# Output projection whole for token blocks 0 to 3 and in two chunks for 4 to 7, with three MLP pairs ahead and two side by side

## The chip, the cores and the metric

The kernel runs on one NeuronCore of a Trainium2 chip. Its time is the device time of one execution in microseconds (us), as the median of several runs. The engines have an instruction queue each and work side by side: TensorE (PE in the profile, its weight loads PEld), VectorE (DVE), ScalarE (ACT), GpSimd (POOL); SyncE (SP) issues the DMA transfers. The program puts the instructions of each engine in one order, and one that waits holds up those behind it on its engine.

## The reference

Two residual layers over 1024 tokens of width 1024, all in float32. Layer 0 mixes with two recurrences, layer 1 with windowed attention; each mixer ends in a projection `m = y @ w_out`, and each layer has an MLP.

```python
for layer in range(DEPTH):                       # DEPTH = 2
    un = rmsnorm(h, g[0])
    m = rec_mixer(un, ...) if layer % 2 == 0 else window_attention(un, ...)
    # both end in: y (1024 x 1024) @ w_out (1024 x 1024)
    h = h + rmsnorm(m, g[1])
    u = rmsnorm(h, g[2])
    m = jnp.square(jax.nn.relu(u @ w1)) @ w2     # w1: 1024 x 4096, w2: 4096 x 1024
    h = h + rmsnorm(m, g[3])
```

## The kernel before

Each large product keeps the precision of float32 by splitting both operands into a rounded high part and the rest (`split`, L84 to L86: ScalarE copies into the rounded type, VectorE subtracts). Three matmuls stand for one: high by high, high by low, low by high. A split therefore costs one ScalarE and one VectorE instruction on each tile, and these two engines prepare what TensorE multiplies.

**Output projection** (`out_proj`). The contraction over 1024 features is cut into 8 tiles k. `hid[k]` is the split transposed mixer output `ys[k]`, `ws[k]` the split weight rows k. For each of 8 blocks b of 128 tokens and each half c of the output columns, `g2_block` (L209) accumulates the products in one PSUM bank. In layer 0, `ys[4]` to `ys[7]` come from the four heads of one of the recurrences, in layer 1 `ys[6]` and `ys[7]` from the last group of attention heads; these are the last to be finished. So the work is in two chunks: k = 0 to 3 for all 8 blocks (12 matmuls for each half block, 192 in all), which can run between the mixer's own matmuls, and then k = 4 to 7 for all 8 blocks. Chunk one is evacuated by ScalarE to `acc` (blocks 0 to 3) or to `far` (blocks 4 to 7, in tiles `ax`, which are copied to `acc` by DMA once `yp` has room); chunk two is added to it by VectorE (L288).

**Norms behind it** (`make_tail`). For each finished block, `add_norm` multiplies by the gain on GpSimd (`mg`, L236), takes the mean square on ScalarE (`junk`, L147) and a Newton step in small VectorE instructions (L148 to L152), adds the residual (`hb`, L238), stores it, and norms it again for the MLP (L147 and then L185, which writes `acc` anew). `turn` transposes a block on TensorE (L191, 8 matmuls of 128 columns into two `aux` banks) and splits it as an operand of the MLP (`xh`, `xl`, and a float32 copy `xf`). Blocks 0 to 3 are turned here, blocks 4 to 7 in the MLP.

**MLP, first product** (`strassen_in`). Hidden columns are handled in 16 pairs p of 128-column slabs. Each pair is a two-by-two Strassen scheme (Winograd's form) of seven products i, each of 12 matmuls of 512 columns. Products 1 and 2 need tokens 0 to 511 only (`p1`, `p2`), the others sums of quarters of the weights (`lead_sums`, `sum_op`, `half`) and of the activations (`acts[3]` to `acts[7]`). Activations 3 and 6 need blocks 4 to 7 turned (`turn_far`), 5 and 7 more sums over them. So the first `lead` pairs do products 1 and 2 while `turn_far` goes on; then their products follow in the order 6, 7, 5, 4, 3 (`rest`). From pair 2 on, a pair runs through 1, 6, 2, 7, 5, 4, 3 while the operands of the next pair are made (`prep_step`).

**PSUM.** Eight banks: two of tag `m0`, two of `m1`, four of `aux`. The out projection uses the `m` banks in turn; `p1` holds an `aux` bank for its pair until `p2` has added product 2 and ScalarE has read it, and every half of a turn takes an `aux` bank.

**Order.** The order of code gives priorities, from which a list scheduler sets the order on every engine at build time; it inserts the semaphores. The mixers have their steps in a string (`REC_ORDER`: `S3` is a stage of head 3, `G3` the gate projection of head 3, `O3` its output). Tiles come from pools: `wp` holds `raw` (2 buffers of freshly loaded weights) and `w1` (3 buffers of split weights), `xp` 8 tiles of 8 KB a partition, `yp` 8 of 4 KB; the pools "op" and "mlp1" are opened and closed in turn over the same memory as the mixers' pools, so a tile of a new pool waits for the last reader of the memory below it.

Of the kernel before, what the change touches and what calls it, by code (L numbers as in the profile page):

```python
# [8 lines left out]
F32 = mybir.dt.float32  # L9
# [9 lines left out]
P = 128  # L19
# [20 lines left out]
             "Z2 G2 S2 z2 s2 G3 !O2 z3 V3 Q3 S3 s3 O3")  # L40
# [11 lines left out]
def trunk_kernel(ctx, tc, x, norm_g, rec_w_in, rec_conv_w, rec_conv_b, rg_w_r, rg_b_r, rg_w_i,  # L52
# [199 lines left out]
    def out_proj(ys, w, h_src, h_dst, layer, nxt, pre):  # L252
# [21 lines left out]
        with phase("op") as pool:  # L274
# [12 lines left out]
            def evac(sl, o):  # L287
                return V.tensor_tensor(acc[b][:, sl], o, acc[b][:, sl], op=ALU.add)  # L288
# [17 lines left out]
    def mlp(xt, hgs, layer, h_src, h_dst, nxt, pre):  # L306
# [3 lines left out]
        def strassen_in(pool):  # L310
# [66 lines left out]
            def prep_step(p, slot):  # L377
# [923 lines left out]
```

## Time and profile before

| | us |
|---|---|
| median of 3 runs | 2274.64 (2272.72 to 2275.8) |
| the profiled execution's own time | 2273.52 |
| its span in the trace | 2271.8 |
| TensorE busy in the span | 2174.1 (96%) |
| VectorE busy | 1728.0 (76%) |
| ScalarE busy | 1145.0 (50%) |
| GpSimd busy | 223.1 (10%) |

TensorE is busy for 96% of the span and for all of the long stretches of the MLPs. A matmul's end is modelled, so the busy share of TensorE is an upper bound; how much a stretch loses is read from the number of matmuls in it and the pace at which they run where nothing waits. A row of the timeline gives the start, the length, engine, line, operation, tiles and shape, how many instructions were merged, and in brackets the engine's idle time before it and what ended it. A row of the table by stretches gives the stretch, its length, then for each engine its busy time and its instructions in it, the clock that TensorE was granted, the DMA share and GB/s.

### The profile page before, as it was taken

Reading aid. Unit: us, or ns where it says so; the run is one execution under the profiler, and the core shown is the slowest. Engines: PE = TensorE matmul, PEld = TensorE weight load, DVE = VectorE, ACT = ScalarE, POOL = GpSimd, SP = SyncE. Lnnn points to the kernel's source line nnn. Section 1 sums busy time; section 2 is a strip of 40 time slices with the busy share of each in tenths; the row PEclk is TensorE's granted clock in tenths of the full one; section 3 lists DMA queues with packets and bytes.
Section 4 is the critical chain, followed back from the end, with each engine's and each line's share of the span. In section 5 each row is a group of like instructions: output and inputs, shape, how many; then the busy total and the mean of one; then the engine's idle time right before and its main releaser. Section 6 shows DMA issues by size and latency. Waiting matters only on the chain. (4 is left out here: it accounts for less than half of the span.)

```text
span 2271.8 us, 28186 instructions
## 1 busy us (share of the span) xinstructions
PE 2174.1 (96%) x10392; PEld 1790.7 (79%) x10392; DVE 1728.0 (76%) x2941; ACT 1145.0 (50%) x1812; POOL 223.1 (10%) x128
## 2 busy tenths in 40 slices
PE   8999999998899999999999888989899999999998
PEld 8878888887788888888878666767678888888886
DVE  6697767758866665778887888997986666578887
ACT  6566445544544456333344665765554445533342
POOL 0230000003000000000022244211200000000003
PEclk9999999999999999999999999999999999999999
DMA  5111011143444446444344112114334443744433
GB/s 148 53 33 56 29 29 30 46 139 121 135 153 153 151 141 255 145 152 153 114 148 125 33 38 56 33 33 152 132 135 153 153 153 136 245 138 153 153 118 129
DMA packets 180764, 264.03 MB, mean 116 GB/s; under 512 B 17041, under 2 KB 98961, under 8 KB 180625
## 3 DMA queue, kind: packets, MB, share of 16 engines
q1 hardware_dynamic: 180624, 262.22, 35.2%
q8 instruction: 82, 1.34, 0.3%
q14 instruction: 58, 0.47, 0.1%
HBM read 179.87 MB, written 70.78 MB: 110 GB/s over the span
## 5 line engine op out<-in xcount | busy, mean ns | idle before, releaser
L116 PE MATMUL m<-xh,w1hl 128*128 128x512 f32 (+1 forms) x1472 | 431.8, 372 | 0.0
L116 PEld LDWEIGHTS m<-xh,w1hl 128*128 128x128 f32 x1472 | 268.9, 193 | 38.1 <-ACT xh L204 0.2
L116 PE MATMUL m<-xl,w1hl 128*128 128x512 f32 (+1 forms) x736 | 274.1, 373 | 0.5 <-DVE xl L205 0.5
L236 POOL TENSOR_TENSOR mg<-acc,g 128x1024 f32<-128x1024 f32 x32 | 82.5, 2577 | 1695.1 <-DVE acc L553 1210.8
L86 DVE TENSOR_TENSOR w1hl<-raw,w1hl 128x1024 fp32r<-128x1024 f32 x108 | 135.9, 1259 | 107.0 <-ACT w1hl L85 106.9
L418 PE MATMUL aux<-xh,w1hl 128*128 128x512 f32 x512 | 169.0, 392 | 0.0
L418 PE MATMUL m<-xh,w1hl 128*128 128x512 f32 x512 | 168.0, 390 | 0.0
L418 PE MATMUL m<-xh,ws 128*128 128x512 f32 x512 | 167.8, 389 | 0.0
L567 ACT ACTIVATE hidh<-hidl 128x1536 fp32r<-128x1536 f32 (+1 forms) x56 | 89.5, 1598 | 145.1 <-DMA hidl<-hs 145.1
L644 PE MATMUL m<-w2h,hidh 128*128 128x512 f32 x416 | 161.8, 389 | 0.0
L644 PE MATMUL m<-w2l,hidh 128*128 128x512 f32 x416 | 161.8, 389 | 0.0
L644 PE MATMUL m<-w2h,hidl 128*128 128x512 f32 x416 | 161.8, 389 | 0.0
L116 PEld LDWEIGHTS m<-xl,w1hl 128*128 128x128 f32 x736 | 142.3, 193 | 19.7 <-DVE xl L205 0.8
L568 DVE TENSOR_TENSOR hidl<-hidl,hidh 128x1536 fp32r<-128x1536 f32 (+1 forms) x56 | 105.9, 1891 | 54.4 <-ACT hidh L567 54.4
L85 ACT ACTIVATE w1hl<-raw 128x1024 fp32r<-128x1024 f32 x116 | 122.4, 1056 | 40.7 <-DMA raw<-in_mlp_w_dram 21.3
L85 ACT ACTIVATE w2h<-b 128x1536 fp32r<-128x1536 f32 (+1 forms) x48 | 76.7, 1599 | 103.7 <-PE m L644 60.6
L85 ACT ACTIVATE ws<-s 128x512 fp32r<-128x512 f32 x88 | 55.7, 634 | 144.6 <-PE m L418 87.2
L644 PE MATMUL aux<-w2h,hidh 128*128 128x512 f32 x312 | 121.4, 389 | 0.0
L644 PE MATMUL aux<-w2l,hidh 128*128 128x512 f32 x312 | 121.4, 389 | 0.0
L644 PE MATMUL aux<-w2h,hidl 128*128 128x512 f32 x312 | 121.4, 389 | 0.0
L418 PEld LDWEIGHTS aux<-xh,w1hl 128*128 128x128 f32 x512 | 96.6, 189 | 20.3 <-ACT u L434 0.4
L418 PEld LDWEIGHTS m<-xh,w1hl 128*128 128x128 f32 x512 | 96.2, 188 | 20.3 <-ACT xh L85 0.4
(298 smaller groups left out, 5152.9 us busy)
## 6 DMA issues: line engine op xcount, KB each, us to landing
hidl<-hs SPq DMA_DIRECT2D x42, 768.0 KB, 4.5
raw<-in_mlp_w_dram SPq DMA_DIRECT2D x30, 1024.0 KB, 5.5
hs<-hid SPq DMA_DIRECT2D x104, 256.0 KB, 2.1
b<-in_mlp_w_dram SPq DMA_DIRECT2D x24, 768.0 KB, 4.8
raw<-in_rec_w_in_dram SPq DMA_DIRECT2D x28, 512.0 KB, 3.7
hidl<-hs SPq DMA_DIRECT2D x14, 1024.0 KB, 5.6
hs<-u SPq DMA_DIRECT2D x52, 256.0 KB, 2.0
hres<-hb SPq DMA_DIRECT2D x24, 512.0 KB, 2.7
```

Of the source, the lines that this page charges most:

```text
L85: A.activation(hi, src, AF.Copy)
L86: (eng or V).tensor_tensor(lo, src, hi, op=ALU.subtract)
L116: T.matmul(o[:, c0:c0 + nw], a[:, k, :], b[k // 4][half][:, k % 4, c0:c0 + nw], start=(n == 0), stop=(n == 3 * KT - 1))
L236: G.tensor_tensor(mg, m, g_post, op=ALU.mult)
L418: T.matmul(o, a[:, k, :], b[:, k, :], start=(first and n == 0), stop=(n == 11), skip_group_check=not first)
L567: A.activation(h, f32(l), AF.Copy)
L568: V.tensor_tensor(l, f32(l), h, op=ALU.subtract)
L644: T.matmul(o, a_[:, j, sl], b_[:, j, :], start=(not more and n == 0), stop=(n == last), skip_group_check=more)
```

## The change

- Output projection: chunk one (k = 0 to 3) is done ahead for blocks 4 to 7 only. Then blocks 0 to 3 are done whole (24 matmuls for each half block, evacuated by ScalarE, no addition on VectorE), and last blocks 4 to 7 get their chunk two. `hid[4]` and `hid[5]` have free tiles early. The copies through `ax` are gone.
- The split weights of the MLP's first slabs are prefetched for three pairs, after block 3; blocks 0 to 3 are turned behind blocks 4 to 6.
- MLP: `lead` is 3. Products 1 and 2 of pairs 0, 1 and 2 run while blocks 4 to 7 are turned. Pairs 0 and 1 then do their remaining products side by side, in the order 3, 5, 6, 7, 4 (`side_by_side`), each product of both pairs behind the making of its operand. Activations 5 and 6 are split in one instruction over 2048 columns each, 6 no longer block by block. The raw weights of pairs 0 and 1 go to tiles of the pool "mlp1" (tags `xh_7`, `xl_7`).
- `G3` moves behind `S3` in the recurrence's order.

The number of TensorE instructions is the same. On VectorE, 16 additions of chunk two are gone (8 in each layer) and 8 splits of 512 columns are replaced by 2 of 2048; ScalarE has 8 evacuations more to `hid` and the same number of out-projection evacuations. SP has 8 transfers less through `ax`.

```diff
-             "Z2 G2 S2 z2 s2 G3 !O2 z3 V3 Q3 S3 s3 O3")
+             "Z2 G2 S2 z2 s2 !O2 z3 V3 Q3 S3 G3 s3 O3")
...
+        def copy(sl, o):
+            return A.activation(acc[b][:, sl], o, AF.Copy)
+
+        def add(sl, o):
+            return V.tensor_tensor(acc[b][:, sl], o, acc[b][:, sl], op=ALU.add)
...
-        acc = [yp.tile([P, D], F32, tag="y", name=f"acc{b}") for b in range(4)]
-        far = []
-        for i in range(2):
-            t = xp.tile([P, 2, S], F32, tag="x", name=f"ax{i}")
-            far += [t[:, b, :] for b in range(2)]
+        acc = {b: yp.tile([P, D], F32, tag="y", name=f"acc{b}") for b in range(4, NB)}
         ws = [load_wo(k, wp, "w1", 3) for k in range(3)] + [load_wo(3, xp, "x", 8)]
-        for b in range(NB):
-            dst = acc[b] if b < 4 else far[b - 4]
-            g2_block(b, [hid[k] for k in range(4)], ws, lambda sl, o: A.activation(dst[:, sl], o, AF.Copy))
+        for b in range(4, NB):
+            g2_block(b, [hid[k] for k in range(4)], ws, copy)
         with phase("op") as pool:
...
-            for b in range(4, NB):
-                acc.append(yp.tile([P, D], F32, tag="y", name=f"acc{b}"))
-                Y.dma_start(acc[b], far[b - 4])
-            ws = [load_wo(k, pool, "wo", 4) for k in range(4, KT)]
-            prefetch(pre)
+            ws += [load_wo(k, pool, "wo", 4) for k in range(4, KT)]
+            acc.update({b: yp.tile([P, D], F32, tag="y", name=f"acc{b}") for b in range(4)})
...
             for b in range(NB):
-                ins = g2_block(b, [hid[k] for k in range(4, KT)], ws, evac)
+                if b < 4:
+                    ins = g2_block(b, [hid[k] for k in range(KT)], ws, copy)
+                else:
+                    ins = g2_block(b, [hid[k] for k in range(4, KT)], ws[4:], add)
                 if b >= 1:
                     add_norm(b - 1, ins)
-                if 2 <= b < 6:
-                    turn(b - 2)
+                if b == 3:
+                    prefetch(pre)
+                if b == 4:
+                    turn(0)
+                if 4 <= b < 7:
+                    turn(b - 3)
...
             def load(p):
...
+                if p < 2:
+                    t = pool.tile([P, KT, 2 * P], F32, tag="x" + "hl"[p] + "_7", name="raw2")
                 else:
...
             def turn_far(b):
...
                 p4 = turned(hgs[b], 1)
-                V.tensor_tensor(t2[:, :, blk], p4, t1[:, :, blk], op=ALU.subtract)
                 A.activation(h3, p4, AF.Copy)
                 V.tensor_tensor(l3, p4, h3, op=ALU.subtract)
-                split(h6, l6, t2[:, :, blk])
+                V.tensor_tensor(t2[:, :, blk], p4, t1[:, :, blk], op=ALU.subtract)
...
+            def side_by_side(p, i):
+                t = temps[p]
+                u2, u3 = t[:, half_s[0]], t[:, half_s[1]]
+                c = lambda h, s: outs[p][h][:, half_s[s]]
+                o = banks[p] if i == 4 else mm_ps({3: "m1", 5: "m0", 6: "aux", 7: "m1"}[i])
+                banks[p] = o
+                product(o, p, i, i != 4, True)
+                if i == 3:
+                    A.activation(c(0, 1), o, AF.Copy)
+                elif i == 5:
+                    outs[p].append(yp.tile([P, S], F32, tag="y", name="hid1"))
+                    A.activation(c(1, 1), o, AF.Copy)
+                    V.tensor_tensor(c(0, 1), o, c(0, 1), op=ALU.add)
+                elif i == 6:
+                    V.tensor_tensor(u2, o, u2, op=ALU.add)
+                    V.tensor_tensor(c(0, 1), c(0, 1), u2, op=ALU.add)
+                    relu2(p, 0, 1, None)
+                elif i == 7:
+                    V.tensor_tensor(u3, o, u2, op=ALU.add)
+                    V.tensor_tensor(c(1, 1), c(1, 1), u3, op=ALU.add)
+                    relu2(p, 1, 1, None)
+                else:
+                    V.tensor_tensor(c(1, 0), o, u2, op=ALU.add)
+                    relu2(p, 1, 0, None)
+                    store(p)
...
-            lead = 2
+            lead, both = 3, (0, 1)
             for p in range(lead):
                 pre_a(p)
-            load(0)
+            for p in both:
+                load(p)
             lead_sums(0)
+            sum_op(0, 3)
...
             p1(0)
+            p1(1)
             turn_far(4)
-            p1(1)
+            p2(0)
             turn_far(5)
-            p2(0)
-            load(1)
-            sum_op(0, 6)
+            p2(1)
             turn_far(6)
-            p2(1)
+            lead_sums(1)
+            sum_op(1, 3)
+            p1(2)
             turn_far(7)
-            lead_sums(1)
-            sum_op(1, 6)
-            for p in range(lead):
-                rest(p, 1)
...
+            p2(2)
+            for p in both:
+                side_by_side(p, 3)
+            act_tiles(5)
+            split(*acts[5], t1)
...
+            for p in both:
+                side_by_side(p, 5)
+            act_tiles(6)
+            split(*acts[6], t2)
...
                            layer, (layer, 2),
-                           [(mlp_w1[layer], 2 * j * P) for j in range(2)])
+                           [(mlp_w1[layer], 2 * j * P) for j in range(3)])
```

What the scheduler makes of it is shown at three places. In these rows the number behind a name tells tiles apart: `m_13512` is a PSUM bank's tile of one half block, `hx_13390` and `hx_13393` are `hid[4]` and `hid[5]` of layer 1, `hidh`/`hidl` are `hid[6]` and `hid[7]`, `wohl` the split weights k = 4 to 7, `w1hl` and `xhl` in the out projection those of k = 0 to 3.

TensorE behind the last attention matmul of layer 1 (`aux<-pl,vs`), before:

```order
L1178 MATMUL aux<-pl,vs 128x512
L216 MATMUL m_13437<-w1hl,hx_13262 128x512
L216 MATMUL m_13437<-w1hl,hx_13265 128x512 x3
L216 MATMUL m_13437<-xhl,hx_13268 128x512 x3
L216 MATMUL m_13451<-w1hl,hx_13259 128x512 x3
L216 MATMUL m_13451<-w1hl,hx_13262 128x512 x3
L216 MATMUL m_13451<-w1hl,hx_13265 128x512 x3
L216 MATMUL m_13451<-xhl,hx_13268 128x512 x3
```

The same place now:

```order
L1211 MATMUL aux<-pl,vs 128x512
L216 MATMUL m_13512<-w1hl,hx_13242 128x512 x3
L216 MATMUL m_13512<-w1hl,hx_13245 128x512 x3
L216 MATMUL m_13512<-xhl,hx_13248 128x512 x3
L216 MATMUL m_13434<-wohl,hx_13390 128x512
L216 MATMUL m_13460<-wohl,hx_13390 128x512
L216 MATMUL m_13486<-wohl,hx_13390 128x512
L216 MATMUL m_13512<-wohl,hx_13390 128x512
L216 MATMUL m_13434<-wohl,hx_13390 128x512 x2
```

Before, 67 matmuls of chunk one (7 of `m_13437`, then 60 of five further half blocks) stand there ahead of the first use of `wohl`; now 9 do, and the four open half blocks of blocks 0 and 1 then take k = 4 to 7 in turns.

ScalarE in layer 1, from the split of `hid[6]` on, before:

```order
L85 ACTIVATE hidh<-y_9688 128x1024
L85 ACTIVATE wohl<-raw 128x1024
L85 ACTIVATE hidh<-y_9689 128x1024
L273 ACTIVATE ax_13275<-m_13451 128x512
L85 ACTIVATE wohl<-raw 128x1024
L273 ACTIVATE ax_13276<-m_13465 128x512
L85 ACTIVATE hx_13524<-y_9686 128x1024
```

The same place now:

```order
L85 ACTIVATE hidh<-y_9668 128x1024
L85 ACTIVATE wohl<-raw 128x1024
L85 ACTIVATE hidh<-y_9669 128x1024
L85 ACTIVATE wohl<-raw 128x1024 x3
L264 ACTIVATE acc_13424<-m_13434 128x512
L264 ACTIVATE acc_13424<-m_13460 128x512
```

The splits of `hid[4]` and `hid[5]` have moved ahead, to between the attention units; the order of `hid[6]`, `hid[7]` and the four `wohl` is kept.

VectorE in layer 1 at the end of the turns of blocks 4 to 7, before (`ws` are split weight sums, `t` the activation sums `t1` and `t2`, `rawy` the raw weights of pair 1, `xl_14146` the low part of activation 6, which the first of the remaining products reads):

```order
L408 TENSOR_TENSOR t_14148<-aux,t_14147 128x4x128
L86 TENSOR_TENSOR ws<-raw_14136,ws 128x512
L406 TENSOR_TENSOR t_14147<-aux,xf_13732 128x4x128
L410 TENSOR_TENSOR xl_14144<-aux,xh_14143 128x4x128
L86 TENSOR_TENSOR xl_14146<-t_14148,xh_14145 128x4x128
L408 TENSOR_TENSOR t_14148<-aux,t_14147 128x4x128
L360 TENSOR_TENSOR s_14280<-rawy 128x512
L86 TENSOR_TENSOR w1hl<-raw_14136,w1hl 128x1024
L410 TENSOR_TENSOR xl_14144<-aux,xh_14143 128x4x128
L86 TENSOR_TENSOR xl_14146<-t_14148,xh_14145 128x4x128
```

The same place now (`raw_14099` and `raw_14101` are the raw weights of pairs 0 and 1; product 3 of pair 0 reads `ws<-raw_14099`, product 3 of pair 1 `ws<-raw_14101`):

```order
L402 TENSOR_TENSOR t_14113<-aux,xf_13815 128x4x128
L359 TENSOR_TENSOR raw_14099<-raw_14099 128x4x128
L356 TENSOR_TENSOR s_14217<-raw_14101 128x512
L405 TENSOR_TENSOR xl_14112<-aux,xh_14111 128x4x128
L357 TENSOR_TENSOR raw_14101<-raw_14101 128x4x128
L406 TENSOR_TENSOR t_14114<-aux,t_14113 128x4x128
L86 TENSOR_TENSOR ws<-raw_14099,ws 128x512
L358 TENSOR_TENSOR raw_14101<-s_14217,raw_14101 128x4x128
L86 TENSOR_TENSOR xl_14298<-t_14113,xh_14297 128x2048
L359 TENSOR_TENSOR raw_14101<-raw_14101 128x4x128
L86 TENSOR_TENSOR xl_14340<-t_14114,xh_14339 128x2048
L86 TENSOR_TENSOR ws<-raw_14101,ws 128x512
```

Product 3 of pair 0 has everything at the seventh of these rows, and between it and the operand of product 3 of pair 1 stand two splits of 2048 columns and two subtractions of 512.

More of the change, by code (lines that the diff above doesn't have):

```diff
@@ L403, in turn_far @@
                 blk = block_cols(b)
[L404 removed]
+                h3, l3 = (t[:, :, blk] for t in acts[3])
                 p4 = turned(hgs[b], 0)
@@ L439, in p2, with store @@
                 relu2(p, 0, 0, banks.pop((p, "a")))
+            def store(p):
+                t = temps[p]
+                u2, u3 = t[:, half_s[0]], t[:, half_s[1]]
+                c = lambda h, s: outs[p][h][:, half_s[s]]
+                if p not in place:
+                    for h in (1, 0):
+                        Y.dma_start(hid_d[2 * p + h], outs[p][h])
+                    return
+                ch, n = place[p]
+                a11, a21, a12, a22 = c(0, 0), c(0, 1), c(1, 0), c(1, 1)
+                s1, s2, s4 = u2, u3, yp.tile([P, 512], F32, tag="y", name="s4")
+                V.tensor_tensor(s1, a21, a22, op=ALU.add)
+                V.tensor_tensor(s2, s1, a11, op=ALU.subtract)
+                V.tensor_tensor(s4, a12, s2, op=ALU.subtract)
+                V.tensor_tensor(a21, a11, a21, op=ALU.subtract)
+                for i, t_ in ((1, a11), (6, s2), (2, a12), (7, a21), (5, s1), (4, a22), (3, s4)):
+                    Y.dma_start(hs_d[ch][i][n], t_)
+            def side_by_side(p, i):
+                t = temps[p]
+                u2, u3 = t[:, half_s[0]], t[:, half_s[1]]
+                c = lambda h, s: outs[p][h][:, half_s[s]]
+                o = banks[p] if i == 4 else mm_ps({3: "m1", 5: "m0", 6: "aux", 7: "m1"}[i])
[19 more added lines that the diff above has]
+                    store(p)
             def rest(p, slot):
@@ L500, in strassen_in @@
-            sum_op(1, 6)
-            for p in range(lead):
-                rest(p, 1)
-            half(0, 1, 7, 4)
+            p2(2)
[4 more added lines that the diff above has]
+            for p in both:
+                sum_op(p, 5)
+            for p in both:
+                side_by_side(p, 5)
+            act_tiles(6)
+            split(*acts[6], t2)
+            for p in both:
+                sum_op(p, 6)
@@ L504, in strassen_in @@
             V.tensor_tensor(b11, t2, b11, op=ALU.subtract)
+            for p in both:
+                half(p, 1, 7, 4)
+            for p in both:
+                side_by_side(p, 6)
             act_tiles(7)
             split(*acts[7], b11)
-            half(1, 1, 7, 4)
-            for p in range(lead):
-                rest(p, 3)
-            sum_op(0, 5)
-            act_tiles(5)
-            split(*acts[5], t1)
-            sum_op(1, 5)
-            for p in range(lead):
-                rest(p, 4)
@@ L516, in strassen_in @@
-            load(2)
             V.tensor_tensor(b21, b21, t2, op=ALU.subtract)
+            for p in both:
+                side_by_side(p, 7)
             acts[4] = x_tile("xh_4"), x_tile("xl_4")
             split(*acts[4], b21)
-            sum_op(0, 3)
-            for p in range(lead):
-                rest(p, 5)
-                prep_step(2, 2 + p)
-            sum_op(1, 3)
+            load(2)
+            prep_step(2, 2)
+            prep_step(2, 3)
+            side_by_side(0, 4)
+            prep_step(2, 4)
@@ L525, in strassen_in @@
             load(3)
-            rest(0, 6)
-            prep_step(2, 4)
-            rest(1, 6)
+            side_by_side(1, 4)
             prep_step(2, 5)
             prep_step(2, 6)
-            for p in range(lead, n_pair):
-                p1(p)
+            for p in range(2, n_pair):
+                if p >= lead:
+                    p1(p)
                 if 4 <= p + 2 < n_pair:
@@ L535, in strassen_in @@
                 for slot in range(1, 7):
-                    if slot == 2:
+                    if slot != 2:
+                        rest(p, slot)
+                    elif p >= lead:
                         p2(p)
-                    else:
-                        rest(p, slot)
                     prep_step(p + 1, slot)
```

37 lines of the change are left out of this document (6 added, 31 removed).

## The prediction

> **What bounds the kernel now.** I read the page's busy shares first, then the chain that ended last, then the matmul counts of stretches around the two out projections, and last the waits in them.
>
> ```profile
> PE 2174.1 (96%) x10392; PEld 1790.7 (79%) x10392; DVE 1728.0 (76%) x2941; ACT 1145.0 (50%) x1812; POOL 223.1 (10%) x128
> 1709.57 10.88 PE m L418 x48
> 440.00:480.00 40.00, 39.77 (x257) 33.36 (x256) 22.06 (x60) 12.69 (x26) 0.00 (x0) 1.00 0.04 14
> 481.69:557.26 75.57, 69.35 (x307) 56.97 (x307) 57.70 (x103) 39.78 (x73) 19.53 (x7) 0.95 0.52 181
> 557.26:578.67 21.41, 15.23 (x81) 11.68 (x79) 19.76 (x37) 14.28 (x27) 3.31 (x1) 0.98 0.36 112
> 578.67:615.70 37.03, 35.54 (x144) 28.59 (x145) 35.72 (x43) 19.96 (x27) 0.00 (x0) 0.92 0.40 135
> 1500.00:1552.12 52.12, 50.67 (x259) 40.11 (x260) 42.96 (x144) 36.25 (x92) 2.57 (x2) 1.00 0.00 1
> 1552.12:1623.26 71.14, 64.68 (x292) 53.00 (x292) 58.01 (x97) 39.06 (x71) 18.17 (x7) 0.98 0.53 185
> 1623.26:1649.19 25.93, 16.90 (x81) 12.79 (x80) 24.34 (x45) 14.74 (x28) 3.16 (x2) 0.88 0.37 112
> 1649.19:1687.50 38.31, 36.27 (x144) 28.84 (x145) 36.16 (x44) 20.08 (x27) 0.00 (x0) 0.90 0.38 131
> ```
>
> TensorE is the bound, and its number of matmuls doesn't change, so only its losses can be won. The second row gives its pace where nothing waits: 10.88 / 48 = 0.2267 us for a matmul of 512 columns. A block's turn of 8 transposes took 0.8 us (one began at 559.83, the next matmul at 560.62).
>
> The rows by stretch cut each transition in three, for layer 0 and layer 1: A, from the mixer's last matmul to the out projection's last; B, from there to the first product that needs blocks 4 to 7 (48 MLP matmuls); C, the 144 MLP matmuls behind it, until 192 are done. A's counts hold 32 transposes and one matmul that only begins in it, so 274 and 259 of the projection; B's hold 48, 32 and one. Losses are the length less count times pace, less 3.2 us for four turns in A and in B:
> A: 75.57 - 62.1 - 3.2 = 10.3 and 71.14 - 58.7 - 3.2 = 9.2.
> B: 21.41 - 10.9 - 3.2 = 7.3 and 25.93 - 10.9 - 3.2 = 11.8.
> C: 37.03 - 32.6 = 4.4 and 38.31 - 32.6 = 5.7.
> Together 22.0 in layer 0 and 26.7 in layer 1: 48.7 us is all that there is to win here.
>
> What TensorE waits for there (timeline of TensorE, its rows with idle time), and the clock around two of these waits and one other:
>
> ```profile
> 522.57 1.27 PE L191 MATMUL aux<-ident,acc 128*128 128x128 f32 x8 [3.66 <-DVE m L148]
> 544.36 1.94 PE L191 MATMUL aux<-ident,acc 128*128 128x128 f32 x8 [2.55 <-DVE acc L185]
> 578.67 0.79 PE L418 MATMUL aux<-xh,ws 128*128 128x512 f32 x1 [4.69 <-ACT xh L85]
> ...
> 1588.42 1.97 PE L191 MATMUL aux<-ident,acc 128*128 128x128 f32 x8 [3.87 <-DVE acc L185]
> 1606.16 1.06 PE L191 MATMUL aux<-ident,acc 128*128 128x128 f32 x8 [2.00 <-DVE acc L185]
> 1632.68 1.11 PE L191 MATMUL aux<-ident,acc 128*128 128x128 f32 x4 [3.09 <-DVE t L406]
> 1649.19 0.79 PE L418 MATMUL aux<-xh,ws 128*128 128x512 f32 x1 [4.93 <-ACT xh L85]
> ...
> 543.83:547.24 3.41, 2.88 (x11) 2.72 (x12) 3.15 (x5) 1.51 (x3) 2.29 (x1) 0.50 0.44 153
> 1604.16:1607.57 3.41, 1.41 (x11) 1.35 (x12) 3.41 (x9) 0.86 (x1) 0.82 (x1) 1.00 0.14 23
> 1646.33:1656.57 10.24, 6.63 (x15) 4.66 (x16) 8.50 (x12) 6.92 (x9) 0.00 (x0) 0.50 0.06 21
> ```
>
> In A, TensorE waits for the norm of a block that it is to turn (L185); in B and C, for the turned blocks' splits. VectorE is behind both: busy 24.34 of 25.93 us in B of layer 1. A wait also costs afterwards: behind an idle time of 2.55 us the granted clock was 0.50 for 3.41 us, behind 2.00 us it stayed 1.00, behind 4.93 us it was 0.50 until 1656.57. A window of 3.41 us at half clock costs 1.7 us of matmuls.
>
> **The change, part by part.** The sum is against the profiled execution (2273.52 us), which is 1.1 us under the median.
>
> *A, blocks 0 to 3 whole.* A block gives TensorE 48 matmuls, 10.9 us, before, 24, 5.4 us; and its first turn stands behind blocks 0 to 4 instead of inside block 2. Block 1's norm has then three blocks, 27 us, of cover; before, block 0's second half was added at 1572.81 and its turn could begin at 1588.42, 15.6 us later. The waits for L185 in A go. Their cover would be gone only if a norm took 27 us. The 8 additions less on VectorE for each layer (0.69 us each) lie in this chain and come on top.
>
> In their place TensorE needs the splits of k = 4 to 7 sooner. Layer 1, where they ended before:
>
> ```profile
> 1554.26 1.05 ACT L85 ACTIVATE hidh<-y 128x1024 fp32r<-128x1024 f32 x1
> 1555.21 1.05 ACT L85 ACTIVATE wohl<-raw 128x1024 fp32r<-128x1024 f32 x1
> ...
> 1563.02 1.06 ACT L85 ACTIVATE wohl<-raw 128x1024 fp32r<-128x1024 f32 x1 [0.50 <-DMA raw<-in_att_w_o_dram]
> 1556.49 1.22 DVE L86 TENSOR_TENSOR wohl<-raw,wohl 128x1024 fp32r<-128x1024 f32 x1
> 1558.76 1.22 DVE L86 TENSOR_TENSOR wohl<-raw,wohl 128x1024 fp32r<-128x1024 f32 x1
> 1564.12 1.23 DVE L86 TENSOR_TENSOR wohl<-raw,wohl 128x1024 fp32r<-128x1024 f32 x1 [1.80 <-ACT wohl L85]
> 1566.91 1.23 DVE L86 TENSOR_TENSOR wohl<-raw,wohl 128x1024 fp32r<-128x1024 f32 x1 [0.20 <-ACT wohl L85]
> 494.92 1.22 DVE L86 TENSOR_TENSOR wohl<-raw,wohl 128x1024 fp32r<-128x1024 f32 x1
> ```
>
> Attention's last matmul ends at 1552.12. Behind it stand 9 matmuls of chunk one and 48 of k = 4 to 7: without a wait, done at 1552.12 + 57 x 0.2267 = 1565.0. If the splits come as before, the last low part is there at 1568.1, and 8 of the last 12 matmuls follow: 1569.9, a loss of 4.9. If the two splits of `hx`, five evacuations and the copies of `ax` that lay between them give back all they can, 1567.2, a loss of 2.2. I take 3.5, the middle, and one window at half clock, 1.7: loss 5.2 instead of 9.2. In layer 0 the last low part comes at 496.1, and TensorE has 13 of chunk one and one more half block between: I take 1.5 instead of 10.3, bounds 0 and 4. Gain in A: 8.8 + 4.0 = 12.8.
>
> *B, three pairs ahead.* TensorE gets 24 matmuls more (5.4 us) while VectorE finishes. VectorE's work from the last eviction to the first product's operand is the same length: before, in layer 1,
>
> ```profile
> 1628.37:1650.68 22.31, 20.75 (x38) 0.83 0.35 106
> L238 DVE SCALAR_TENSOR_TENSOR hb<-mg,r,hb 128x1024 f32<-128x1024 f32 x8 | 12.4, 1552 | 0.4
> 1658.77 2.29 DVE L86 TENSOR_TENSOR xl<-xf,xh 128x2048 fp32r<-128x2048 f32 x1
> 1642.26 0.68 DVE L86 TENSOR_TENSOR xl<-t,xh 128x512 fp32r<-128x512 f32 x1
> 1642.86 0.68 DVE L410 TENSOR_TENSOR xl<-aux,xh 128x512 fp32r<-128x512 f32 x1
> ```
>
> 22.3 us, VectorE busy for 20.75 of it. The tail of two norms stays. Of the rest, 17 instructions of 512 columns and one of 1024 (1.1 us) before: the four subtractions for activation 6 go, pair 0's sums come behind the turns and one more weight split ahead, which makes 19 of 512. At one each 0.60 us (1642.26 to 1642.86), 19 x 0.60 = 11.4 against 17 x 0.60 + 1.1 = 11.3. So B keeps its 21.4 and 25.9 us, with 72 matmuls in it: gain 5.4 in each layer, 10.8. Bounds: 0 if B grows by the same 5.4, and 19.1 if B loses nothing. The raw weights of pairs 0 and 1 now lie where `hid[6]` and `hid[7]` lay and can only be fetched behind block 7. Two transfers of 1024 KB, each 5.5 us to landing,
>
> ```profile
> raw<-in_mlp_w_dram SPq DMA_DIRECT2D x30, 1024.0 KB, 5.5
> ```
>
> are there 12 us behind block 7 at the latest; VectorE comes to them some 15 us behind it, since 8 of those 19 and the two norms come first: nothing.
>
> *C, side by side.* Product 3 of pair 1 reads an operand that stands five VectorE instructions behind that of pair 0: three of 0.60, two of 2.2, 6.2 us, while TensorE has 2.7 us for product 3 of pair 0. So it waits 3.5 us, with a window at half clock, 1.7. Then seven products follow, 19 us, while VectorE has 16.5 us of operands for them; I put 1.0 for hand-overs. C loses 6.2 instead of 4.4 and 5.7: -2.3. Bounds: no loss, +10.1; and VectorE late throughout, with 7% of idle time as in the row above, -8.
>
> *Moved into the mixers.* In layer 1 two splits (ScalarE 1.05, VectorE 1.23) move between the last attention units, where VectorE is busy 42.96 of 52.12 us: between 0 and 2.5, I take 1.0. `G3` changes place in a stretch in which TensorE is busy 39.77 of 40 us: nothing to win; two table loads more on the way to `s3` would cost 2.6, a fill that came better 0.2: I take 1.0, as it now must end before `s3`'s exponentials.
>
> The sum: -12.8 - 10.8 + 2.3 + 2.0 = -19.3: 2273.5 - 19.3 = 2254.2, and against the median 2274.6 - 19.3 = **2255.3 us**.
>
> [...]
>
> **Rivals.**
> 1. *VectorE stays late through C.* Behind product 3 of pair 0 it has 22.7 us of work until the operand of product 4, TensorE 21.8 us of matmuls: no reserve. If each of the eight products waits for its operand, C costs 8 more in the two layers and B wins half: 2255.3 + 8 + 5.4 = 2269. For it speaks the busy share of 0.94 in B; against it that VectorE is busy 35.7 of 37.0 us in C before, with waits of TensorE of 2 us only.
> 2. *The turns of blocks 4 to 7 go one by one* (this one ends slower). `p1` of three pairs holds up to three of the four `aux` banks; with one bank left, each half of a turn takes TensorE 0.66, ScalarE 0.60 and VectorE two of 0.69 before the next: 2.64 us, 21.1 for eight, against 10.8 in my sum. That is 10.3 for each layer and two half-clock windows each, 20.6 + 6.8: 2282.7. It decides from 2.5 us a half on. Against it: the order puts `p1(2)` behind block 6's turn, when `p2` has freed two banks; and in the trace halves begin 1.4 us apart (1640.30, 1641.68) with two free:
>
> ```profile
> 1640.30 0.60 PE L191 MATMUL aux<-ident,acc 128*128 128x128 f32 x4
> 1641.68 0.66 PE L191 MATMUL aux<-ident,acc 128*128 128x128 f32 x4
> ```
>
> 3. *The cover is complete*: no wait left in A and B, C as forecast: 48.7 - 6.2 x 2 = 36.3 less 2.0: 2240. For it, nothing but that TensorE has more to do; against it, VectorE's 22.3 us behind the last eviction.
>
> **How the numbers follow.** A measurement of this kernel tells about 0.2%, 4.5 us, from no change. The forecast, 2248 to 2263 by its bounds in A and C, has 0.52. Rival 1: 0.21, of which a third within 4.5 us of no change. Rival 2: 0.16; a weak form of it (half the price) ends within 4.5 us, 0.06, the rest slower. Rival 3: 0.11. So faster 0.52 + 0.14 + 0.11 = 0.77, same 0.13, slower 0.10. The range of 8 in 10 goes from halfway to rival 3 to rival 1: 2245 to 2270.
>
> **What would show it.** In the changed profile: no idle time before turns in A; a wait for `wohl` of 2 to 5 us behind attention's last matmul, under 2 us in layer 0; B as long as before with 72 matmuls; a wait of about 3.5 us in the second product on `ws`, released by VectorE L86. The forecast is wrong if TensorE waits for turns of blocks 4 to 7 for more than before, if waits stand before each of products 5, 6, 7 and 4, or if the mixers' ends come more than 3 us later.

## The result, and the profile after

The changed kernel took 2249.09 us (median of 4, 2247.71 to 2250.35) against 2274.04 us before in the same series (median of 4): a ratio of 0.989, 95% interval 0.9873 to 0.9907. That is 25 us less; forecast were 19.3 less, 2255.3 us, in a range of 2245 to 2270. The profiled execution took 2248.92 us, its span is 2247.2.

The stretches are cut as in the prediction. A runs from the mixer's last matmul to the out projection's last, B to the first product on `ws`, C until 192 MLP matmuls are done (120 of them now, as 72 lie in B). The columns are start and end, length, busy time and count of TensorE's matmuls, of its weight loads, of VectorE, ScalarE and GpSimd, then granted clock, DMA share and GB/s:

```profile
PE 2165.5 (96%) x10392; PEld 1781.8 (79%) x10392; DVE 1706.2 (76%) x2923; ACT 1146.1 (51%) x1814; POOL 223.5 (10%) x128
479.12:548.62 69.50, 69.47 (x319) 56.49 (x318) 43.82 (x79) 36.15 (x66) 15.17 (x7) 1.00 0.43 144
548.62:573.65 25.03, 21.22 (x105) 16.55 (x104) 23.49 (x48) 16.35 (x31) 6.48 (x2) 1.00 0.52 178
573.65:604.43 30.78, 28.61 (x121) 22.16 (x121) 30.70 (x34) 19.48 (x27) 0.00 (x0) 1.00 0.30 102
1541.07:1605.65 64.58, 61.29 (x282) 49.62 (x281) 44.75 (x82) 36.49 (x67) 15.67 (x7) 1.00 0.47 156
1605.65:1632.07 26.42, 22.44 (x104) 17.75 (x104) 23.33 (x48) 16.03 (x31) 6.27 (x2) 0.94 0.49 167
1632.07:1662.90 30.83, 28.59 (x122) 22.13 (x121) 30.75 (x34) 19.48 (x27) 0.00 (x0) 1.00 0.30 102
```

With 0.2267 us for a matmul and 0.8 us for a turn, the losses are, in A, 69.50 - 286 x 0.2267 - 3.2 = 1.5 and 64.58 - 249 x 0.2267 - 3.2 = 4.9; in B, with 72 matmuls, 5.5 and 6.9; in C 30.78 - 27.2 = 3.6, twice. Together 26.0 us, where 48.7 were lost before. The rest of the 24.6 us between the two spans is outside these stretches. Layer 0's mixer ends 2.57 us sooner now, with 12 matmuls of the out projection fewer done in it (2.7 us of work). From C of layer 0 to layer 1's last attention matmul it is as long as before (936.4 and 936.6 us), with 10 more of them done in it.

A good part of the gain is clock. Before, nine windows of 3.41 us in A, B and C ran at a granted clock of 0.50, and TensorE was busy for 24.8 us of them; half of that, 12.4 us, is my estimate of what half clock cost of the 48.7. Now there is one such window (1620.04 to 1623.45, 1.7 us). So some 10.7 of the 22.7 us won here are matmuls that no longer run slowly behind a wait, and the other half are the waits themselves.

TensorE's waits that are left in layer 1, from the timeline (start, duration, then in brackets the idle time before and what ended it):

```profile
1545.19 1.19 PE L216 MATMUL m<-wohl,hx 128*128 128x512 f32 x4 [2.03 <-ACT wohl L85]
1546.63 4.83 PE L216 MATMUL m<-wohl,hx 128*128 128x512 f32 x20 [0.26 <-DVE wohl L86]
1552.40 1.75 PE L216 MATMUL m<-wohl,hidh 128*128 128x512 f32 x5 [0.94 <-ACT wohl L85]
1607.05 0.50 PE L413 MATMUL aux<-xl,w1hl 128*128 128x512 f32 x1 [1.18 <-DVE xl L205]
1614.13 0.50 PE L413 MATMUL aux<-xh,w1hl 128*128 128x512 f32 x1 [0.68 <-ACT u L429]
1619.04 0.66 PE L191 MATMUL aux<-ident,acc 128*128 128x128 f32 x4 [1.90 <-DVE t L402]
...
1633.05 0.73 PE L413 MATMUL m<-xh,ws 128*128 128x512 f32 x2 [0.28 <-DVE ws L86]
1637.19 0.50 PE L413 MATMUL m<-xh,ws 128*128 128x512 f32 x1 [1.59 <-ACT ws L85]
1639.26 0.73 PE L413 MATMUL m<-xh,ws 128*128 128x512 f32 x2 [0.29 <-DVE ws L86]
```

The waits for norms (L185) ahead of the turns in A are gone. What stands there now is the wait for the splits of `wohl` behind attention, 3.2 us in three pieces; in layer 0 A has no wait at all (TensorE busy 69.47 of 69.50 us). In B one half turn waits 1.90 us for VectorE, and behind it no idle time over 0.3 us is left before the first product on `ws`.

### The profile page after: what moved, and what is told of

The parts are those of the page before. It is cut to its first block, busy times and chain, and to the rows that moved or that the text cites. A ratio compares the mean times of both kernels' runs of the same rounds, so it can differ in the third digit from the quotient of the medians.

```text
span 2247.2 us, 28124 instructions
## 1 busy us (share of the span) xinstructions
PE 2165.5 (96%) x10392; PEld 1781.8 (79%) x10392; DVE 1706.2 (76%) x2923; ACT 1146.1 (51%) x1814; POOL 223.5 (10%) x128
## 4 chain that ended last, share of the span: by engine, by line
PE 74%; DVE 17%; ACT 5%; issue 2%; DMA 2%; POOL 0%; SPq 0%; DVEq 0%; ACTq 0%; POOLq 0%
PE m L413 14%; PE m L677 13%; PE m L116 11%; PE aux L413 10%; PE aux L677 9%; PE m L216 8%; DVE sm L1200 1%; PE aux L1205 1%; DVE hb L238 1%; DVE w1hl L86 1%; PE aux L948 1%; DVE acc L185 1%; ACT sm L1196 1%; DVE sm L1186 1%; DVE e L151 1%
## 5 line engine op out<-in xcount | busy, mean ns | idle before, releaser
L116 PEld LDWEIGHTS m<-xh,w1hl 128*128 128x128 f32 x1472 | 267.9, 193 | 38.2 <-ACT qf L1107 0.5
L85 ACT ACTIVATE w1hl<-raw 128x1024 fp32r<-128x1024 f32 x118 | 124.1, 1054 | 33.5 <-DMA raw<-in_mlp_w_dram 11.5
L413 PEld LDWEIGHTS m<-xh,ws 128*128 128x128 f32 x512 | 95.8, 188 | 28.4 <-ACT ws L85 5.5
```

The source lines that it names most:

```text
L85: A.activation(hi, src, AF.Copy)
L116: T.matmul(o[:, c0:c0 + nw], a[:, k, :], b[k // 4][half][:, k % 4, c0:c0 + nw], start=(n == 0), stop=(n == 3 * KT - 1))
L413: T.matmul(o, a[:, k, :], b[:, k, :], start=(first and n == 0), stop=(n == 11), skip_group_check=not first)
```

## The experiments

A difference of a few us between whole runs can come from elsewhere: the stretch from C of layer 0 to layer 1's last attention matmul (the rest of the MLP and the mixer), whose matmuls are the same in all these kernels up to some 10 of the out projection, took from 933.6 to 940.7 us in the profiles. So the verdicts rest on the losses of A, B and C, worked out from each profile as above (us):

| kernel | layer 0: A, B, C | layer 1: A, B, C | sum |
|---|---|---|---|
| before | 10.3, 7.3, 4.4 | 9.2, 11.8, 5.7 | 48.7 |
| changed | 1.5, 5.5, 3.6 | 4.9, 6.9, 3.6 | 26.0 |
| out projection's part alone | 2.8, 8.7, 5.8 | 5.7, 8.7, 5.0 | 36.7 |
| MLP's part alone | 3.3, 6.8, 5.3 | 6.9, 8.8, 4.8 | 35.9 |
| before, sums held back | 7.3, 9.4, 4.2 | 4.6, 12.2, 4.4 | 42.1 |
| changed, two pairs ahead | 1.5, 9.2, 3.8 | 4.9, 9.6, 4.5 | 33.5 |
| changed, G3 back | 0.7, 5.3, 3.6 | 5.8, 5.7, 3.6 | 24.7 |
| changed, w_o split first | 1.4, 5.3, 3.6 | 3.7, 6.0, 3.6 | 23.6 |
| both of these | 2.0, 5.4, 3.6 | 4.1, 5.3, 3.6 | 24.0 |
| changed, eight sums on GpSimd | 0.8, 9.4, 0.5 | 4.8, 9.7, 0.6 | 25.8 |
| changed, pair 1's sums on GpSimd | 0.7, 5.4, 4.9 | 5.9, 5.2, 6.4 | 28.5 |
| changed, pair 1's sums on GpSimd and both small edits | 1.8, 5.5, 7.2 | 3.6, 5.5, 6.4 | 30.0 |
| the same, raw weights on GpSimd's queue | 1.8, 6.5, 1.9 | 3.9, 6.0, 5.1 | 25.2 |

**The out projection's part alone.** `out_proj` of the changed kernel with `for j in range(2)` in its last argument, everything else as before.

> The kernel before with the out projection's part of the change alone (blocks 0 to 3 whole; two pairs ahead, old order of the products, G3 where it was). Theory 1, that the two parts act in their own stretches: A falls from 75.6 to about 69.5 us in layer 0 and its loss from 9.2 to about 4.9 in layer 1, B and C stay as before; with the 2 us that layer 1's mixer won, 13 to 15 us less than before: 2259 to 2261. Theory 2, that the first part also clears B, because VectorE's additions are gone and the norms of blocks 6 and 7 come free of long VectorE instructions: B loses at least 4 us less in layer 1, and the whole change but C's gain is already there: 18 to 22 us less, 2252 to 2256.

It took 2261.53 us, ratio 0.9947 (0.9935 to 0.9959), 12.7 us less. A lost 11.0 us less, B and C together 1.0 less: theory 1 holds in the sum. B of layer 1 did lose 3.1 less, as theory 2 had it, but B and C of layer 0 lost 2.8 more.

**The MLP's part alone.** The changed `strassen_in` and `for j in range(3)`, on the out projection as before.

> The kernel before with the MLP's part alone (three pairs ahead, two side by side in operand order; out projection in two chunks for all blocks). Theory 1: A as before (losses 10.3 and 9.2), B takes 72 matmuls in about the length it has now, C's loss is 3.6 in each layer: 9 to 10 us less than before, 2264 to 2265. Theory 2: B still holds the long VectorE instructions that it had before (3.52 and 3.42 us in layer 1) and wins less than 3 us: 4 to 6 us less in all, 2268 to 2270.

It took 2258.29 us (2253.11 to 2261.98), ratio 0.9931 (0.9918 to 0.9943): 16.0 us less than the 2274.26 before in that series, and more than either theory gave. 12.7 + 16.0 is more than the whole change brings (by the losses 12.0 + 12.8 against 22.7), so the parts share a gain. It lies in A, whose code this kernel doesn't touch: A lost 3.3 and 6.9 us instead of 10.3 and 9.2. What differs there is on VectorE. Its timeline in A of layer 0 before, around the first block's norm:

```profile
509.76 0.78 DVE L360 TENSOR_TENSOR s<-raw 128x512 f32<-128x512 f32 x1 [1.01 <-DMA raw<-in_mlp_w_dram]
510.47 0.68 DVE L288 TENSOR_TENSOR acc<-m,acc 128x512 f32<-128x512 f32 x1
511.07 0.68 DVE L361 TENSOR_TENSOR raw<-raw 128x512 f32<-128x512 f32 x1
511.67 0.15 DVE L150 RECIPROCAL y<-s 128x1 f32<-128x1 f32 x1
511.78 0.69 DVE L362 TENSOR_TENSOR raw<-s,raw 128x512 f32<-128x512 f32 x1
512.39 0.21 DVE L151 SCALAR_TENSOR_TENSOR e<-y,m 128x1 f32<-128x1 f32 x1
512.52 0.68 DVE L363 TENSOR_TENSOR raw<-raw 128x512 f32<-128x512 f32 x1
513.12 0.68 DVE L288 TENSOR_TENSOR acc<-m,acc 128x512 f32<-128x512 f32 x1
513.72 0.15 DVE L152 SCALAR_TENSOR_TENSOR r<-e,y 128x1 f32<-128x1 f32 x1
513.96 3.39 DVE L238 SCALAR_TENSOR_TENSOR hb<-mg,r,hb 128x1024 f32<-128x1024 f32 x1
```

L360 to L363 are the four sums of MLP pair 0 (`lead_sums`). The raw weights of pair 0 lay in a buffer of tag `w1`, which is free once chunk one of the out projection is done with it, and the scheduler put the sums here, in the middle of block 0's norm; VectorE waited 1.01 us for the weights, with the norm queued behind. The MLP's part moves the raw weights into memory that block 7 frees, and the sums with them to B.

**The sums held back.** The kernel before with one order added on VectorE:

```diff
-                V.tensor_tensor(t, a21, a22, op=ALU.add)
+                ins = V.tensor_tensor(t, a21, a22, op=ALU.add)
+                if p == 0:
+                    tc.add_manual_dep(ins.ins, mm_state['normed'].ins.name,
...
+                                      reason="sums behind the last norm")
```

`mm_state['normed']` is the last instruction of the last block's norm; the dependency is one of order only.

> The kernel before with one order added on VectorE: the first of pair 0's four sums (L360) stands behind the norm of the last block, where it stood inside the out projection, ahead of block 0's norm. Nothing else is changed: all blocks in two chunks, two pairs ahead, old order of the products. Theory 3, formed on the traces of the two halves of the change: A's waits before came from these sums, which put 2.7 us of VectorE's work and a wait of 1.0 us for the raw weights in front of block 0's norm; A's loss falls to some 3.5 us in layer 0 and 6.7 in layer 1 as in the run of the MLP's part, and B grows by up to 2.4 in each layer: 4 to 9 us less than before, 2265 to 2270. Theory 1, as the prediction had it: the waits come from the short blocks, A loses as before and B grows: 0 to 5 us more, 2274 to 2279.

It took 2266.21 us, ratio 0.9959 (0.9946 to 0.9971): 8.5 us less than the 2274.69 of its series, with no block whole, no third pair and the old order. The same instruction of block 0's norm in its timeline:

```profile
510.67 1.28 DVE L238 SCALAR_TENSOR_TENSOR hb<-mg,r,hb 128x1024 f32<-128x1024 f32 x1
```

It is done at 511.95 instead of 517.35. 2.1 of these 5.4 us are the excess of the row at 513.96 over 1.28 (last section). A lost 7.6 us less, B 2.5 more: theory 3. The gain isn't the sums' own time alone, since with the new order such an excess also shrank, in the rows from 500 to 535 us from 3.4 us (at 513.96 and 523.26) to 2.2 (at 525.41); the two aren't told apart here.

Layer 0's A still loses 7.3 us, not 3.5, with waits of 1.89 and 2.49 us for block norms; behind the second, at 533.66, six matmuls took 2.54 us, where six took 1.52 to 1.64 before it. The short blocks, theory 1's cause, are still there, but that they alone make these waits is not shown. In the norm behind the second stands

```profile
525.41 3.48 DVE L238 SCALAR_TENSOR_TENSOR hb<-mg,r,hb 128x1024 f32<-128x1024 f32 x1
```

2.2 us above its usual 1.28. The MLP's part alone has the same long instruction (3.48 us at 524.35), but waits of only 0.41 and 1.94 us, and the granted clock over A was 1.00. At the first wait TensorE came to the turn 1.0 us later than here, and the norm was done 0.5 us sooner.

**Two pairs ahead.** In the changed kernel `lead = 2`, without `p1(2)` and `p2(2)`, two prefetches.

> The changed kernel with two pairs ahead instead of three; pairs 0 and 1 still side by side. Theory 1, VectorE sets B's length: B stays 25 to 26 us with 48 matmuls instead of 72, so the 24 matmuls (5.4 us) come back in each layer: 9 to 11 us slower than the changed kernel, 2258 to 2260, and TensorE waits in B for some 5 us more. The rival, B's length follows TensorE's own work (B grew by 3.6 us in layer 0 when it got 5.4 us of matmuls): B falls back to 21 to 22 us, 1 to 4 us slower than the changed kernel, 2250 to 2253.

2256.1 us, ratio 0.9928 (0.9915 to 0.9941): 7 us slower than the changed kernel, between the two theories. Two windows of B answer it, layer 0 and layer 1:

```profile
549.08:572.38 23.30, 15.14 (x82) 12.04 (x80) 21.46 (x44) 14.30 (x27) 3.96 (x2) 0.93 0.44 147
1608.73:1632.39 23.66, 15.14 (x81) 12.04 (x80) 21.45 (x44) 14.30 (x27) 3.96 (x2) 0.97 0.44 145
```

B gets 1.7 and 2.8 us shorter, not 5.4, and TensorE's busy share falls to 65 and 64%: VectorE sets B's length. What little went is mostly VectorE's arrears: without the third pair's weight split in A the last eviction ends 4.2 us behind A's end, with it 5.7 and 5.5. Of the 10.8 us of matmuls that the third pair puts into the two B, some 6 are free of charge.

**G3's place.** First in the kernel before (`s2 G3 !O2` to `S3 G3 s3`), then back in the changed one.

> The kernel before with G3 moved behind S3 in the recurrent mixer's order and nothing else. The price in the prediction's sum was 1.0 us; theory 1, read from the changed kernel's trace, is 0 (within 0.3 us in the stretch up to the mixer's last matmul): 2274. The rival, two table loads more on the way to s3: 2.6 us slower, 2276.7.

> The changed kernel with G3 back in its old place in the recurrent mixer's order. If the place of G3 is worth nothing, as the mixer's own stretch says (0.15 us): 2249 within 1.5 us. If the 3 us less that the kernel before showed with G3 moved come from the mixer's end, they are lost again here: 2251 to 2253. If they came from another timing of the raw weights against the first norms in A, which the changed kernel doesn't have, nothing again: 2249.

Moved in the kernel before: 2271.17 us, ratio 0.9987 (0.9976 to 0.9997), which neither 2274 nor 2276.7 had foreseen; of this run only whole times are used. Moved back in the changed kernel: 2247.32 us, ratio 0.9879 (0.9866 to 0.9893), where the changed one has 0.989, again just under every expectation. Moving it brought 3 us in one and cost 1.8 in the other, each hardly clear of the interval: nothing is shown but that it is small.

**w_o's first splits ahead.**

```diff
+            ws += [load_wo(k, pool, "wo", 4) for k in (4, 5)]
             for k in (6, 7):
                 ... split(*hid[k], ys[k])
-            ws += [load_wo(k, pool, "wo", 4) for k in range(4, KT)]
+            ws += [load_wo(k, pool, "wo", 4) for k in (6, 7)]
```

> The changed kernel with the splits of w_o's k = 4 and 5 written ahead of the splits of hid[6] and hid[7]. Theory: the wait of 2.03 us behind attention's last matmul is there because ScalarE splits hid[7], which needs the last unit's output, before it splits w_o; with w_o's splits ahead of it the wait goes and A loses 2 to 3 us less in layer 1, nothing changes in layer 0: 2246 to 2247. Rival: the tiles for these splits lie in memory that attention holds until its end, so that they can't be written sooner: within 1 us of the changed kernel.

2247.07 us, ratio 0.9883 (0.9868 to 0.9898). The waits of 2.03 and 0.26 us became one:

```profile
1544.52 6.09 PE L216 MATMUL m<-wohl,hx 128*128 128x512 f32 x24 [1.10 <-ACT wohl L85]
1551.56 1.76 PE L216 MATMUL m<-wohl,hidh 128*128 128x512 f32 x5 [0.94 <-ACT wohl L85]
```

A of layer 1 lost 1.2 us less, half of what was expected; by the whole time it can't be told from the changed kernel.

**Both small edits together.**

> The changed kernel with w_o's first two splits ahead of those of hid[6] and hid[7], and G3 in its old place. If the two small gains measured apart (2.0 and 1.8 us) are real and independent: 2245 within 1 us. If the second was run-to-run spread of the mixers (their stretches of one and the same work differed by up to 2 us between profiles): 2247.

2247.22 us, ratio 0.988 (0.9867 to 0.9893): no more than the first alone. It is one of the three fastest here, and none of the three is clear of the changed kernel.

**The eight sums on GpSimd.** `e = G if p in (0, 1) else V` in `lead_sums`.

> The changed kernel with the eight sums of pairs 0 and 1 on GpSimd instead of VectorE. Theory: VectorE sets B's length, and 8 instructions of 0.60 us less on it (4.8 us in each layer) bring 2.5 to 4.5 us in each: 5 to 9 us less than the changed kernel, 2240 to 2244. Rival 1: VectorE's long instructions run 2.1 us longer whenever GpSimd works beside them, as two did in the changed kernel; three or four such in each layer take the gain away: 2248 to 2254. Rival 2: B is set by the chain of the last two norms, not by VectorE's sum of work: within 1 us.

2251.03 us, ratio 0.9897 (0.9884 to 0.9911), no gain. The time lies in the range of rival 1, but for another reason. C's loss went from 3.6 to 0.5 and 0.6; B's grew from 5.5 and 6.9 to 9.4 and 9.7. GpSimd's timeline in layer 1:

```profile
1613.11 3.27 POOL L236 TENSOR_TENSOR mg<-acc,g 128x1024 f32<-128x1024 f32 x1 [2.62 <-DVE acc L267]
1625.01 1.29 POOL L357 TENSOR_TENSOR s<-raw 128x512 f32<-128x512 f32 x1 [8.63 <-DMA raw<-in_mlp_w_dram]
...
1629.11 2.12 POOL L360 TENSOR_TENSOR raw<-raw 128x512 f32<-128x512 f32 x1
```

The sums wait for the raw weights and then take 1625.01 to 1631.23; the first product's operand is made from the last of them. On VectorE they are shorter and stand among its other work, and there the last one ended about as late: 24.3 us behind A's end in the changed kernel, 23.8 here (22.9 and 23.3 in layer 0). So the late sums alone don't lengthen B. What does is the order on ScalarE, from its timeline and TensorE's here:

```profile
1631.26 0.63 ACT L85 ACTIVATE ws<-raw 128x512 fp32r<-128x512 f32 x1 [2.50 <-POOL raw L360]
1631.80 0.58 ACT L430 ACTIVATE u<-aux 128x512 f32<-128x512 f32 x1
1632.43 0.79 PE L414 MATMUL aux<-xh,w1hl 128*128 128x512 f32 x1 [3.09 <-ACT u L430]
```

The split of `ws` waits for GpSimd's last sum, and behind it stands the copy `u` of pair 2, which product 2 of that pair needs; in the changed kernel `u` came ahead of the split, at 1628.59. So TensorE stood still for 3.09 us (2.91 in layer 0) in front of 12 matmuls, and the first product on `ws` came behind them, at 1636.67. What an order with `u` first would bring is not shown.

Why the weights come so late is in SyncE's queue of the changed kernel:

```profile
1606.42 10.41 SPq L243 DMA_DIRECT2D hres<-hb  x3
1616.93 1.47 SPq L323 DMA_DIRECT2D raw<-in_mlp_w_dram  x2
1625.57 0.68 DVE L356 TENSOR_TENSOR s<-raw 128x512 f32<-128x512 f32 x1
```

Block 7's last matmul, the last reader of their memory, ends at 1605.65, but on the queue they stand behind the store of the last block's residual: issued 11.3 us later.

**Pair 1's sums alone on GpSimd, alone and with the two small edits, and with the raw weights on GpSimd's queue.** `e = G if p in (1,) else V`; in the last one also `(G if p < 2 else Y).dma_start(t, ...)`.

> The changed kernel with the four sums of pair 1 alone on GpSimd; those of pair 0 stay on VectorE. In the run with all eight sums there, B grew by 3 to 4 us, since pair 0's raw weights landed 17 us behind block 7 and GpSimd took 6.2 us for the four sums ahead of the first product's operand; C's loss fell from 3.6 to 0.5. If C's loss comes from pair 1's operand standing behind VectorE's other work, C keeps that gain here and B stays as in the changed kernel: 4 to 6 us less, 2243 to 2245. Rival, that VectorE's instructions of 2048 columns get longer beside GpSimd (3.38 us against 2.29 for one in that run): B and C give back what C won, 2248 to 2251.

> The three together: pair 1's sums on GpSimd, w_o's first splits ahead, G3 in its old place. If they act in their own stretches (C, A of layer 1, A of layer 0), the sum of what each brings: 2239 to 2242. If GpSimd's work costs what C wins: 2245 to 2247.

> As the run before, and the raw weights of pairs 0 and 1 fetched by GpSimd's queue instead of SyncE's, where they stand behind the store of the last block's residual and are issued 11 us behind block 7's last matmul. By GpSimd they can go behind its last product with g, some 2 us sooner. If B waits for raw weights, 1 to 3 us less than the run before. If B is VectorE's own work, the same within 1 us; if issuing them holds GpSimd up, up to 3 us more.

2248.99 us, ratio 0.989 (0.9877 to 0.9904); 2253.87 (2246.08 to 2255.48), ratio 0.9901 (0.9886 to 0.9915); 2249.29, ratio 0.9888 (0.9875 to 0.9902). None is faster. Pair 1 waits longer, not shorter; from the first of the three:

```profile
1632.43 0.50 PE L414 MATMUL m<-xh,ws 128*128 128x512 f32 x1 [3.37 <-ACT ws L85]
```

Its four sums took GpSimd from 1624.59 to 1631.71, and C lost 4.9 and 6.4 us. So C's gain with all eight sums there was B's loss: its first product on `ws` began at 1636.67, here at 1628.32, and pair 1 had the time between. With both small edits C lost 7.2 and 6.4. With GpSimd's queue the losses are 6.5 and 6.0 in B and 1.9 and 5.1 in C; GpSimd's sums began 20.6 us behind A's end, against 20.9 and 21.3 in the two runs with SyncE's queue: no sooner start worth the name.

## Why the prediction was right, step by step

*A: right in size, with a reason that is only part of it.* Forecast 8.8 + 4.0; it was 8.8 + 4.3. The reason given was that blocks of 48 matmuls cover the norms, and 11.0 us came with whole blocks alone in the first experiment. But the step missed that the waits of before had a second cause. The sums of pair 0 were counted into B's 19 instructions, and never taken out of A, though the order of the kernel before had them there and the trace shows them. Holding them back alone brings 7.6 us of the same 13.1. The first experiment isn't free of this cause: whole blocks read the `w1` buffers until block 3, so the sums stand in A there too, but at 528.9 us in layer 0, behind the norms of blocks 0 to 2, instead of at 509.8 in that of block 0. How much is the cover's and how much the sums' is not shown. A third share is the excess of VectorE's instructions beside GpSimd (last section): 16.4 us in A before, 7.0 now.

The wait for `wohl` in layer 1 came as forecast, 3.2 us against 3.5. In layer 0 the number agrees by luck: the 1.5 us charged were for such a wait, and the 1.5 us lost hold none. The half-clock window charged in layer 1 (1.7 us) did not come: the granted clock over A is 1.00. The waits there were pieces of 2.03 us at most. That too may be luck: over A of layer 1 the granted clock was 0.97 with two pairs ahead, whose `out_proj` is the same, and 0.97 with the out projection's part alone.

*B: the step that failed.* Forecast were 5.4 + 5.4 us; it was 1.8 + 4.9. "B keeps its 21.4 and 25.9 us" took VectorE's work behind the last eviction as equal, and that was right: 19 instructions of 512 columns there, as counted, and 20.2 and 20.8 us before, 19.4 and 20.9 now, from the eviction's end to the first product on `ws`. But the sum was made from A's end. The last eviction of the out projection, before and after, layer 0 and layer 1:

```profile
557.74 0.68 DVE L288 TENSOR_TENSOR acc<-m,acc 128x512 f32<-128x512 f32 x1
1627.69 0.69 DVE L288 TENSOR_TENSOR acc<-m,acc 128x512 f32<-128x512 f32 x1
```

```profile
553.62 0.68 DVE L267 TENSOR_TENSOR acc<-m,acc 128x512 f32<-128x512 f32 x1
1610.45 0.68 DVE L267 TENSOR_TENSOR acc<-m,acc 128x512 f32<-128x512 f32 x1
```

A ended at 557.26 and 1623.26, now at 548.62 and 1605.65: the eviction was done 1.2 and 5.1 us behind it, now 5.7 and 5.5. In layer 0, with 4.5 us more of arrears and 0.9 less of its own stretch, B grew by 3.6 us: so much of A's gain there was handed on to it. VectorE's rows of before, from the end of A, say where the arrears were:

```profile
549.14 0.69 DVE L288 TENSOR_TENSOR acc<-m,acc 128x512 f32<-128x512 f32 x1 [0.98 <-PE m L216]
554.58 0.69 DVE L288 TENSOR_TENSOR acc<-m,acc 128x512 f32<-128x512 f32 x1 [0.44 <-PE m L216]
...
1613.32 2.35 DVE L152 SCALAR_TENSOR_TENSOR r<-e,y 128x1 f32<-128x1 f32 x1
1621.63 3.52 DVE L185 SCALAR_TENSOR_TENSOR acc<-hb,r,g 128x1024 f32<-128x1024 f32 x1
```

In layer 0 VectorE had caught up and waited for matmuls. In layer 1, where TensorE had waited as well, it had not: two of its instructions had taken 4.4 us more than usual beside GpSimd. That VectorE catches up while TensorE waits, and is late when the waits go, fits layer 0, but no run shows it by itself.

*C: wrong sign.* Forecast -2.3, it was +2.9 (4.4 and 5.7 lost before, 3.6 each now). By the estimate above 5.9 of the 10.1 us lost before were half clock; now none is, at a granted clock of 1.00 in both layers. The term that was mis-sized is the wait of product 3 of pair 1: 3.5 us and a window at half clock were charged; the rows above have 1.59 us, released by ScalarE's high part, and 0.29 for VectorE's low part. The count of five VectorE instructions ahead was right (1632.91 to 1638.52), but the product needs the low part late: at 1637.19 the order begins with matmuls on the high part. In layer 0 the wait was 1.51 us; neither cost clock. Behind it no wait over 0.3 us was left in C, so rival 1 fell: VectorE is busy 30.7 of 30.8 us and still in time.

*The mixers.* 2.0 us were charged. Layer 0's cost 0.15; the stretch with layer 1's came out 2 us better, less than it differs from kernel to kernel (7 us). The charge is neither confirmed nor refuted.

*Rivals 2 and 3.* The far turns did not go one by one: one half turn waits 1.90 us (1.53 in layer 0), where the price was 10.3 for each layer. The cover is not complete: 12.4 us are still lost in B.

*The raw weights* "there 12 us behind block 7 at the latest" was wrong: issued 11.3 us behind it, behind a store that waits for the last norm, a queue that the step had not looked at. It was hidden by little: VectorE came to them 8.6 us after their issue, and where GpSimd waited for them, in the run with all eight sums there, it began 6.6 us after their issue at 1618.41.

So the sum came out 5 us short by errors that partly cancel: A +0.3, B -4.1, C +5.2, mixers +3.9.

## What to carry to other kernels

Look at what else stands in the order of an engine that is waited for: four instructions of the next stage, put there because their data happened to be ready, held up the norms, and holding them back brought 7.6 us where whole blocks brought 11.0. When a wait goes, ask how far behind the other engine is at the end of the stretch; measure its work from its own last instruction, not from the first engine's. And before work is moved to an idle engine, follow the chain that feeds it and the one behind it: the weights stood late in a DMA queue, and ScalarE waited for the slower sums with a copy behind it that TensorE needed; VectorE's relief did not decide.

## What the runs showed of the hardware that was not expected

Some of VectorE's instructions took longer beside a product with g on GpSimd. In B of layer 1 before:

```profile
1628.54 3.42 DVE L238 SCALAR_TENSOR_TENSOR hb<-mg,r,hb 128x1024 f32<-128x1024 f32 x1
1628.51 2.36 POOL L236 TENSOR_TENSOR mg<-acc,g 128x1024 f32<-128x1024 f32 x1 [4.46 <-issue]
```

GpSimd ended at 1630.87 and VectorE 1.09 us behind it, almost the whole of its usual 1.28. In A and B of the kernel before, ten VectorE instructions took over 0.8 us more than the median of their kind, each beside a product with g on GpSimd: 19.9 us in all.

Three of them are norm instructions of L185 and L238 (3.39, 3.52 and 3.42 us), and most of the others are Newton steps (L151, L152) that take 0.16 to 0.22 us otherwise and up to 2.45 here. In the changed kernel there are four, all Newton steps in A, 7.0 us. The two "long instructions" that the expectation of the run with eight sums on GpSimd counts in the changed kernel are such steps (2.40 and 2.39 us); all its norm instructions took 1.27 to 1.29. Nor is it every overlap: six norm instructions of the kernel before lay beside GpSimd for some 1.05 us and kept their length. On GpSimd, with all eight sums there, the product at 1613.11, begun beside a norm instruction of VectorE (1612.88 to 1614.15), took 3.27 us, the one at 1598.51 2.40. The 22.3 us from which the prediction sized B in layer 1 held the 2.1 us of excess of the row at 1628.54.

And a wait shorter than those named in the prediction cost clock. Two neighbouring windows of the changed kernel's TensorE, around the half turn that waited 1.90 us (length, busy time and count, granted clock):

```profile
1616.60:1620.04 3.44, 1.54 (x11) 1.00 0.78 222
1620.04:1623.45 3.41, 3.41 (x12) 0.50 1.08 368
```

Behind 1.90 us of idle time the clock was 0.50 for 3.41 us; behind 2.03 us at 1543.16, and behind 1.53 us at the same place of layer 0, it stayed 1.00. So the length of the wait alone does not tell whether the clock falls. In the 3.41 us ahead of this half clock TensorE was busy for 1.51 us, ahead of the six stretches at half clock in A, B and C of the kernel before for 0 to 1.39 us (1.39 with the wait of 2.55 us that the prediction names, 540.42 to 543.83). In the 3.41 us up to the end of the wait of 2.03 us it was 1.38, and the clock stayed 1.00: what decides is not shown.
